# The first mixer of a two-block kernel: the convolution's projections ahead, the inverse's rows ahead of the token-major operands, fox in steps

## The chip, the cores and the metric

One core of a Trainium2 chip runs the whole kernel in one launch. The core has a matmul engine (PE, TensorE, with its weight loads shown apart as PEld), a vector engine (DVE), an activation engine (ACT), a general engine (POOL, GpSimd) and a queue engine that issues transfers (SP). Each engine works through its own list of instructions in order, and waits on semaphores for the others. The metric is the device time of one execution in microseconds, here the median over several runs. TensorE's clock is granted by the chip: 1.00 in the profile's column PEclk is 2.4 GHz, 0.50 is 1.2 GHz.

## What is computed

Two blocks one after the other on x, 256 tokens of 1024 values, in fp32. The first block has two layers, and each begins with the mixer that the change is about:

```python
def hybrid_mixer(x, w_in, mix_scale, w_out, gdn_conv_w, gdn_a_log, gdn_dt_bias, gdn_norm_w,
                 cnv_dw_w, cnv_dw_b, cnv_ln_g, cnv_ln_b, fox_f_bias):
    proj = jnp.einsum('btd,de->bte', x, w_in)
    (a_q, a_k, a_v, a_decay, a_beta, a_gate, c_glu, f_q, f_k, f_v, f_forget) = split_columns(proj, IN_SIZES)
    qkv = jax.nn.silu(causal_depthwise_conv(jnp.concatenate([a_q, a_k, a_v], -1), gdn_conv_w))
    ...
    o_a = gated_delta_rule(heads(a_q, GDN_HEADS), heads(a_k, GDN_HEADS), heads(a_v, GDN_HEADS), log_decay, beta)
    ...
    glu_a, glu_b = jnp.split(c_glu, 2, axis=-1)
    u = glu_a * jax.nn.sigmoid(glu_b)
    u = causal_depthwise_conv(u, cnv_dw_w) + cnv_dw_b          # 31 taps
    o_b = jax.nn.silu(layer_norm(u, cnv_ln_g, cnv_ln_b))
    ...
    o_c = forgetting_attention(heads(f_q, FOX_HEADS), heads(f_k, FOX_HEADS), heads(f_v, FOX_HEADS), log_f)
    mixed = jnp.concatenate([o_a, o_b, o_c], axis=-1) * mix_scale
    return jnp.einsum('bte,ed->btd', mixed, w_out)
```

Three branches share one projection: the gated delta rule with 6 heads of 64 (its per-chunk part inverts a unit lower triangular matrix of 64 x 64 and then runs a recurrence over four chunks of 64 tokens), a long depthwise convolution with 31 taps over 256 channels, and forgetting attention with 6 heads ("fox"). Behind each mixer stand layer norms and a feed-forward part, dense in the first layer and a mixture of experts in the second; the second block of two layers follows and is not touched.

## The kernel before, in words

Tokens lie along the free axis in most tiles: a projection matmul has 128 output columns of the weight as its stationary operand, and 256 tokens as the moving one. Weights come as a stream of pieces of 128 columns by SP's queue. A piece marked 'w' in `WHOLE` goes to PE as it came, in fp32 (operand `raw`, or `x,raw` in the mixer); a piece marked 'p' is split into a high part (`hi`, on ACT) and a rest (`lo`, on DVE), and takes three quicker matmuls (`xh,hi`, `xl,hi`, `xh,lo`), called projection matmuls below.

`_mixer1` (line 724) runs at 0 to 240 us for layer 0 and at 430 to 660 us for layer 1. It first projects k and q with their short convolution, then `gdn` (line 922) takes over: decays and a first gram matrix, the token-major operands `kbe`, `kd`, `vb` (keys and values transposed and scaled), then the inverse. The inverse has two parts: 16 *rows* of its 16 x 16 diagonal blocks (lines 1003 to 1021: POOL builds `dd`, PE spreads it, DVE makes a product `xpr` and sums it into `xt`, one row behind the other), and *levels* that double the block's size (from line 1024 on: transposes `cst,XT`, matmuls `xt,A`, `xc,A`, `zc,X` of 16 or 32 columns). A second pair of decays and gram matrix with q follows, then `u` and `wT` (matmuls `vb,XT` and `XT,kbe`), and the recurrence over four chunks (`S,wT`, `vn,kd`, `dec,vn`, `qg,S`). `fox` (line 1186) works head by head: scores from four operands (`cr,selt`, `selt,cr`, `mkb,identb`, `fb`), a softmax on ACT and DVE, transposes `cst,fp` and matmuls `fpT,fv`. `conv_taps` (line 1161) steps the 31 taps of the long convolution (`cvacc`, DVE), `conv_norm` (line 1174) normalizes it (`ps_st`, `ln_r`, `ln_mr`).

All other work of the mixer is put between these steps by hand. `fill(...)` (line 817) reads letters from a table `FILL`, one per layer, at marks in the code: 'c' draws the next pieces of the projection stream, a digit draws that many steps of the convolution's taps, 'U' loads and 'u' multiplies a part of the second block's memory projection (`ps_mm<-raw`). The order of the program made in this way is the priority by which a scheduler sets each engine's list. Before, `fox` is called whole behind `gdn`.

## Time and profile before

| | us |
|---|---|
| median of the runs | 2953.21 (2950.23 to 2973.36) |
| profiled execution, time | 2977.77 |
| profiled execution, span of its instructions | 2976.0 |
| PE busy | 2914.9 (98%) |
| DVE busy | 2161.2 (73%) |
| ACT busy | 1753.1 (59%) |
| POOL busy | 77.8 (3%) |

The mean granted clock of the span is 0.976. The profile is read in three steps: the busy shares and the chain tell which engine sets the end; the windows tell PE's busy time and clock in each stretch; the timeline gives the durations of single instructions. In a group like `ps_sm<-xt,A 128x16 x12` the result stands left of the arrow and the operands right; an fp32 matmul appears as two records, so x12 is six matmuls. An interval in brackets is the engine's idle time before it, with the instruction that ended it.

### The profile page before, as it was taken

The page shows a single profiled execution, that of the slowest core. Times are in us where ns is not written, and L with a number is a line of the kernel's source. Part 1 is how long each engine was busy: PE and PEld are TensorE (multiplying, and loading weights), DVE is VectorE, ACT ScalarE, POOL GpSimd, SP SyncE. Part 2 cuts the span into 40 slices and gives each one's busy share as a digit, 9 for nine tenths or more (in the row PEclk, how much of TensorE's full clock was granted, in tenths as well). Part 3 has the DMA queues.
Part 4 walks back from the last instruction along what each step waited for, and adds up shares of the span by engine and source line. Part 5 has one row for each costly group of instructions (what it writes and reads, how often), then busy time and mean ns, then how long its engine had stood idle before and what let it go on. Part 6 is the DMA issues. An engine that isn't in the chain of part 4 may idle for free.

```text
span 2976.0 us, 48787 instructions
## 1 busy us (share of the span) xinstructions
PE 2914.9 (98%) x19525; PEld 2642.4 (89%) x19525; DVE 2161.2 (73%) x3156; ACT 1753.1 (59%) x2576; POOL 77.8 (3%) x142
## 2 busy tenths in 40 slices
PE   8999999999999999999999999999999999999998
PEld 7889998888788787788888899989999999989998
DVE  5466556649888898898988866676766665767764
ACT  4245444448787776778777754565554444665543
POOL 1100001000000000000000000100000000100000
PEclk9799999899999999999999999999999999999999
DMA  5224533229989998898999755534655555435553
GB/s 196 82 103 167 200 135 114 91 79 359 361 327 357 364 356 315 335 349 343 354 364 365 269 201 186 192 107 150 217 184 187 184 186 194 146 102 197 206 186 113
DMA packets 104205, 663.77 MB, mean 223 GB/s; under 512 B 11808, under 2 KB 17952, under 8 KB 28576
## 3 DMA queue, kind: packets, MB, share of 16 engines
q1 hardware_dynamic: 101664, 658.46, 60.2%
q8 instruction: 156, 2.56, 0.3%
q10 hardware_dynamic: 2304, 2.10, 0.2%
q14 instruction: 81, 0.66, 0.1%
HBM read 657.36 MB, written 3.15 MB: 222 GB/s over the span
## 4 chain that ended last, share of the span: by engine, by line
PE 57%; DVE 2%; ACT 1%; issue 0%; POOL 0%; POOLq 0%; DVEq 0%; ACTq 0%
PE ps_mm L216 47%; PE py L216 5%; PE ps_fx L216 2%; PE ps_sm L216 2%; DVE lo L205 1%; PE ps_fx L226 0%; PE ps_sm L226 0%; DVE aa L1776 0%; ACT hi L201 0%; DVE gi L205 0%; PE ps_st L216 0%; DVE aa L205 0%; ACT xr L202 0%; DVE y L213 0%; DVE ffab L205 0%
## 5 line engine op out<-in xcount | busy, mean ns | idle before, releaser
L205 DVE TENSOR_TENSOR lo<-raw,hi 128x1024 fp32r<-128x1024 f32 (+2 forms) x1216 | 1435.1, 1207 | 392.2 <-ACT hi L201 378.4
L201 ACT ACTIVATE hi<-raw 128x1024 fp32r<-128x1024 f32 (+2 forms) x1216 | 1247.1, 1044 | 637.5 <-PE ps_mm L216 474.1
L216 PE MATMUL ps_mm<-xh,hi 128*128 128x256 f32 x2736 | 776.9, 284 | 13.2 <-ACT hi L201 8.2
L216 PE MATMUL ps_mm<-xh,lo 128*128 128x256 f32 x2736 | 771.9, 283 | 2.1 <-DVE lo L205 2.1
L216 PE MATMUL ps_mm<-xl,hi 128*128 128x256 f32 x2736 | 772.5, 282 | 0.0
L216 PEld LDWEIGHTS ps_mm<-xh,hi 128*128 128x128 f32 x2736 | 520.3, 190 | 19.4 <-ACT hi L201 8.9
L216 PEld LDWEIGHTS ps_mm<-xh,lo 128*128 128x128 f32 x2736 | 519.5, 190 | 6.0 <-issue 3.3
L216 PEld LDWEIGHTS ps_mm<-xl,hi 128*128 128x128 f32 x2736 | 520.9, 190 | 3.2 <-issue 2.9
L216 PE MATMUL ps_mm<-lo,xgh 128*128 128x512 f32 x896 | 356.8, 399 | 0.7
L216 PE MATMUL ps_mm<-hi,xgl 128*128 128x512 f32 x896 | 350.0, 391 | 0.0
L216 PE MATMUL ps_mm<-hi,xgh 128*128 128x512 f32 x896 | 349.5, 392 | 0.0
L216 PE MATMUL ps_mm<-ffl,hi 128*128 128x256 f32 x880 | 246.8, 280 | 0.0
L216 PE MATMUL ps_mm<-ffh,hi 128*128 128x256 f32 x880 | 246.7, 280 | 0.0
L216 PE MATMUL ps_mm<-ffh,lo 128*128 128x256 f32 x880 | 246.7, 280 | 0.0
L216 PEld LDWEIGHTS ps_mm<-lo,xgh 128*128 128x128 f32 x896 | 168.4, 188 | 48.5 <-DVE lo L205 16.4
L216 PEld LDWEIGHTS ps_mm<-hi,xgh 128*128 128x128 f32 x896 | 168.5, 188 | 35.6 <-ACT hi L201 0.2
L216 PEld LDWEIGHTS ps_mm<-hi,xgl 128*128 128x128 f32 x896 | 168.7, 188 | 32.4
L216 PE MATMUL py<-lo,hh 128*128 128x512 f32 x448 | 178.5, 398 | 0.5
L216 PE MATMUL py<-hi,hl 128*128 128x512 f32 x448 | 174.8, 392 | 0.5
L216 PEld LDWEIGHTS ps_mm<-ffl,hi 128*128 128x128 f32 x880 | 166.6, 189 | 0.0
L216 PEld LDWEIGHTS ps_mm<-ffh,hi 128*128 128x128 f32 x880 | 166.5, 189 | 0.0
L216 PEld LDWEIGHTS ps_mm<-ffh,lo 128*128 128x128 f32 x880 | 166.5, 189 | 0.0
(432 smaller groups left out, 3762.5 us busy)
## 6 DMA issues: line engine op xcount, KB each, us to landing
raw<-in_sm SPq DMA_DIRECT2D x336, 1024.0 KB, 6.5
raw<-in_s SPq DMA_DIRECT2D x248, 1024.0 KB, 4.8
raw<-in_s SPq DMA_DIRECT2D x40, 512.0 KB, 3.4
raw<-in_s SPq DMA_DIRECT2D x32, 256.0 KB, 2.7
raw<-in_mem SPq DMA_DIRECT2D x5, 1024.0 KB, 4.9
kv<-kvt ACTq DMA_DIRECT2D x16, 128.0 KB, 2.1
raw<-kv SPq DMA_DIRECT2D x16, 128.0 KB, 2.8
raw<-in_s SPq DMA_DIRECT2D x2, 1005.0 KB, 6.8
```

The costliest lines, as they stand in the source:

```text
L201: return self.nc.scalar.activation(out, in_, func, scale=scale, **kw)
L205: return self.nc.vector.tensor_tensor(out=out, in0=a, in1=b, op=op)
L216: return self.nc.tensor.matmul(out, lhsT=l, rhs=r, start=start, stop=stop, skip_group_check=True, **kw)
```

## The change

It replaces the two tables `FILL` by one and adds a row `REST` that is played behind `gdn`; the order of the projections changes; in `gdn` the code of the inverse's rows is moved ahead of the exponentials and transposes of the token-major operands; `fox` becomes a generator of ten steps (letter 'x') that writes its result to a tile of its own, which is split later; a tile of the softmax becomes smaller. Line numbers after are one higher from line 164 on, up to the moved code.

```diff
-FILL = ({'s': 'cccc', 'g': 'ccccccc', 'i3': 'cccc', 'f20': '3', 'f00': '2', 'v0': 'U', 'f11': '6', 's2': 'u', 'f10': '4', 's1': 'u'}, {'s': 'cccc', 'g': 'ccccccc', 's1': 'cccc8', 'i1': 'cccc', 'f21': '6', 'z': '1', 's3': 'cc8', 'w': 'u', 'i5': 'U', 's2': 'u'})
+FILL = {'s': 'cccc', 'g': 'cccccccc', 'd': 'cccccc'}
+REST = 'ccccx3cc3x3x3x3Ux3x3x3ux3x3x3ccccu999'
...
-        pp = self.ph.tile([128, 2, T], F32, name="fp", tag="fp", bufs=2)
+        n0, nn = segs[0][1], sum(n for _, n in segs)
+        pb = self.ph.tile([128, nn], F32, name="fp", tag="fp", bufs=2)
+        pp = [pb[:, :n0], pb[:, n0:]]
...
-        rest = cols('fq', 3) + cols('fk', 3) + cols('gate', 3)
-        cl = [cols('v', 3)[:2], cols('v', 3)[2:], cols('gb', 2), cols('ga', 2)] + [rest[i:i + PG] for i in range(0, 9, PG)]
+        qk = cols('fq', 3) + cols('fk', 3)
+        cl = [cols('gb', 2), cols('ga', 2), cols('v', 3)[:2], cols('v', 3)[2:]] + [qk[i:i + PG] for i in range(0, 6, PG)]
+        cl += [cols('gate', 3)[:2], cols('gate', 3)[2:]]
...
+                elif n == 'x':
+                    next(box['fox'], None)
...
+        fo = self.sb([3, T], "fo")
+        box['fox'] = self.fox(l, fq, fk, fv, logf, fo)
         oS = self.gdn(l, qkv, lr, g, lnb, fill)
-        fill('c' * 40)
-        fill('9999')
-        fill(FILL[l].get('z', ''))
-
+        fill(REST)
         mh, ml = self.new_hl()
-        self.fox(l, fq, fk, fv, logf, mh, ml, fill)
-        fill(FILL[l].get('n', ''))
+        for i in range(3):
+            self.split(mh[:, 5 + i], ml[:, 5 + i], fo[:, i])
         self.conv_norm(l, G)
...
         L = gram(decay(0, "mL", rL), k)
-        fill(FILL[l].get('d', ''))
+
+
+        six = lambda a: a.rearrange("p a i c -> p (a i) c")
...
+        self.tt(dl, d16, dl, ALU.subtract)
+        xt = self.ph.tile([128, 12, 16], F32, name="xt16", tag="xt16", bufs=1)
+        nc.vector.tensor_copy(out=xt, in_=d16)
+        fill(FILL.get('d', ''))
+        prod = self.ph.tile([128, 12 * 16], F32, name="xpr", tag="xpr", bufs=1)
+        for i0 in range(0, 16, 2):
...
 
         self.act(ex[:, :, 0:6], rL, AF.Exp)
...
-    def fox(self, l, fq, fk, fv, logf, mh, ml, fill):
+    def fox(self, l, fq, fk, fv, logf, fo):
...
+        yield
         for i in range(3):
...
                 PT.append(self.softmax_T(segs))
-                fill(FILL[l].get(f'f{i}{par}', ''))
+                yield
...
-            self.split(mh[:, 5 + i], ml[:, 5 + i], po, self.p(f"mix_scale{l}", 5 + i))
+            self.act(fo[:, i], po, AF.Copy, scale=self.p(f"mix_scale{l}", 5 + i))
+            yield
```

How the engines' lists change is shown at three places of layer 0; layer 1 is almost alike. A line is: source line, operation, result and operands, size, and how many of them follow each other.

DVE's list at the start of the inverse's rows. Before:

```order
L205 TENSOR_TENSOR xpr<-ps_sm,xt_631 128x24
L1021 TENSOR_REDUCE xt_631<-xpr 128x12
L205 TENSOR_TENSOR xpr<-ps_sm,xt_631 128x36
L1021 TENSOR_REDUCE xt_631<-xpr 128x12
L205 TENSOR_TENSOR xpr<-ps_sm,xt_631 128x48
```

DVE's list at the same place, after (`cacc` and `qkv` are the short convolution of v, `cvacc` the long one's taps):

```order
L206 TENSOR_TENSOR xpr<-ps_sm,xt_579 128x36
L214 SCALAR_TENSOR_TENSOR cacc<-craw,gch_157,cacc 128x254
L1007 TENSOR_REDUCE xt_579<-xpr 128x12
L214 SCALAR_TENSOR_TENSOR cvacc<-uu,cdwh_368,cvacc 128x250
L214 SCALAR_TENSOR_TENSOR cacc<-craw,gch_157,cacc 128x253
L206 TENSOR_TENSOR xpr<-ps_sm,xt_579 128x48
L214 SCALAR_TENSOR_TENSOR cvacc<-uu,cdwh_368,cvacc 128x249
L1007 TENSOR_REDUCE xt_579<-xpr 128x12
```

The rows stood back to back; now each product and each sum has up to two operations of the two convolutions behind it, and further down `kbe`, `kd` and `vb` stand among the last rows. On PE, 144 projection matmuls stand between the eight `dd` and ahead of the first level, where raw matmuls of the memory's projection stood.

PE's list in the levels, from the first 16-column matmuls of the second half on. Before:

```order
L226 MATMUL ps_sm<-cst,XT 128x128 x3
L216 MATMUL ps_sm<-xt_631,A 128x16 x6
L216 MATMUL ps_mm<-x,raw 128x256 x2
L216 MATMUL ps_sm<-zc,X 128x16 x6
L226 MATMUL ps_sm<-cst,XT 128x128 x3
L216 MATMUL ps_mm<-x,raw 128x256
L226 MATMUL ps_sm<-cst,XT 128x128 x3
L216 MATMUL ps_sm<-xc,A 128x32 x6
```

PE's list there, after:

```order
L217 MATMUL ps_sm<-zc,X 128x16 x6
L227 MATMUL ps_sm<-cst,XT 128x128 x3
L217 LDWEIGHTS identb
L217 MATMUL ps_mm<-mkb,identb 128x128
L217 MATMUL ps_mm<-fb 128x128
L217 MATMUL ps_mm<-cr,selt 128x256
L227 MATMUL ps_sm<-cst,XT 128x128 x3
L217 MATMUL ps_sm<-xt_579,A 128x16 x6
L217 MATMUL ps_mm<-selt,cr 128x256
```

The raw matmuls between the levels have been replaced by the four kinds of score matmuls of `fox`; two and a half heads stand in the levels, one and a half in the decays and gram that follow.

PE's list in the second gram matrix and behind it, where the levels have ended. Before:

```order
L216 MATMUL ps_sm<-qkv 128x128 x3
L216 MATMUL ps_mm<-xl,hi 128x256
L216 MATMUL ps_mm<-xh,lo 128x256
L216 MATMUL ps_sm<-rows,selt 128x256
L216 MATMUL ps_mm<-xh,hi 128x256
L216 MATMUL ps_mm<-xl,hi 128x256
L216 MATMUL ps_mm<-xh,lo 128x256
L216 MATMUL ps_mm<-xh,hi 128x256
L216 MATMUL ps_sm<-rows,selt 128x256 x2
```

PE's list there, after:

```order
L217 MATMUL ps_sm<-qkv 128x128 x6
L217 MATMUL ps_mm<-raw 128x256
L217 MATMUL ps_sm<-qkv 128x128 x3
L217 MATMUL ps_sm<-rows,selt 128x256
L227 MATMUL ps_fx<-cst,fp 128x128 x3
L217 MATMUL ps_fx<-fpT,fv 64x128
L217 MATMUL ps_sm<-rows,selt 128x256 x2
L217 MATMUL ps_fx<-fpT,fv 64x128 x2
```

Sixteen projection matmuls stood between the second decays and the `XT,kbe` matmuls; now pieces of `fox` stand there. In the recurrence that follows, 54 projection matmuls have been replaced by `cst,fp`, `fpT,fv` and 16 raw ones. The last two heads stand behind the recurrence, then the gate's 48 projection matmuls, 24 raw ones, and the convolution's statistics, with 8 projection matmuls between the last of these (`zq`) and `ln_r`.

## Rows read from the trace of the kernel before

**Rows 1.** Page, busy time (us, share, instructions) and chain by engine:
```profile
PE 2914.9 (98%) x19525; PEld 2642.4 (89%) x19525; DVE 2161.2 (73%) x3156; ACT 1753.1 (59%) x2576; POOL 77.8 (3%) x142
...
PE 57%; DVE 2%; ACT 1%; issue 0%; POOL 0%; POOLq 0%; DVEq 0%; ACTq 0%
```

**Rows 2.** Waits of PE, first and second execution: us in total, times, longest:
```profile
PE ps_sm L216 <- POOL dd L1011: 2.1, 2, 1.9
...
PE ps_sm L216 <- POOL dd L1011: 3.7, 1, 3.7
```

**Rows 3.** Windows, first execution; columns in the first row:
```profile
core 0: us, PE busy (x) PEld busy (x) DVE busy (x) ACT busy (x) POOL busy (x), PEclk, DMA share, GB/s
...
87.00:98.30 11.30, 11.30 (x83) 10.33 (x82) 4.78 (x6) 4.59 (x9) 3.95 (x2) 1.00 0.52 186
98.30:132.40 34.10, 34.10 (x136) 30.34 (x136) 12.70 (x23) 9.23 (x26) 0.00 (x0) 0.50 0.21 78
132.40:172.00 39.60, 39.60 (x333) 35.10 (x333) 30.25 (x75) 16.94 (x31) 0.00 (x0) 1.00 0.19 67
172.00:200.00 28.00, 27.27 (x176) 21.14 (x174) 15.82 (x50) 13.90 (x42) 2.06 (x3) 1.00 0.29 114
```

**Rows 4.** Windows, second execution, same columns:
```profile
505.00:521.00 16.00, 15.41 (x61) 11.21 (x62) 10.64 (x35) 2.00 (x2) 6.29 (x8) 0.80 0.40 155
...
528.00:549.00 21.00, 21.00 (x89) 19.27 (x87) 8.21 (x18) 4.21 (x10) 1.64 (x1) 0.51 0.02 5
...
603.00:617.00 14.00, 14.00 (x50) 9.80 (x51) 4.23 (x17) 4.90 (x19) 0.00 (x0) 0.52 0.10 40
```

**Rows 5.** Timeline of PE: start, duration, operation; levels at two clocks:
```profile
94.78 1.41 PE L216 MATMUL ps_sm<-xt,A 128*128 128x16 f32 x12
...
530.15 2.58 PE L216 MATMUL ps_sm<-xt,A 128*128 128x16 f32 x12
```

**Rows 6.** Timeline of DVE: operands, inverse's rows, convolution taps, a weight's split:
```profile
65.59 0.55 DVE L205 TENSOR_TENSOR kd<-ps_sm,ex 128x384 f32<-128x384 f32 x1
...
76.28 0.18 DVE L205 TENSOR_TENSOR xpr<-ps_sm,xt 128x24 f32<-128x24 f32 x1 [3.29 <-PE ps_sm L216]
...
85.85 0.35 DVE L1021 TENSOR_REDUCE xt<-xpr 128x12 f32<-128x192 f32 x1
...
162.20 10.12 DVE L213 SCALAR_TENSOR_TENSOR cvacc<-uu,cdwh,cvacc 128x239 f32<-128x239 f32 x27
...
173.52 2.35 DVE L205 TENSOR_TENSOR lo<-raw,hi 128x1024 fp32r<-128x1024 f32 x2
```

**Rows 7.** Timeline of PE: `dd`, two heads' starts in fox, projection matmuls:
```profile
78.38 0.81 PE L216 MATMUL ps_sm<-dd,cst 128*128 128x384 f32 x2
...
178.47 0.38 PE L216 MATMUL ps_mm<-cr,selt 128*128 128x256 f32 x1
...
180.50 0.38 PE L216 MATMUL ps_mm<-cr,selt 128*128 128x256 f32 x1
...
195.95 0.28 PE L216 MATMUL ps_mm<-xh,hi 128*128 128x256 f32 x1
196.07 0.28 PE L216 MATMUL ps_mm<-xl,hi 128*128 128x256 f32 x1
```

**Rows 8.** Windows, matmuls and splits of raw alone, columns as above:
```profile
87.30:98.30 11.00, 5.22 (x21) 3.49 (x20) 2.45 (x2) 2.11 (x2) 0.00 (x0) 1.00 0.53 191
98.30:116.80 18.50, 7.29 (x14) 4.09 (x14) 2.44 (x2) 2.09 (x2) 0.00 (x0) 0.50 0.23 86
```

**Rows 9.** Timeline of PE and of DVE: the convolution's statistics and norm:
```profile
176.01 0.58 PE L216 MATMUL ps_st<-cst,zq 128*128 128x1 f32 x4
...
180.09 0.16 DVE L213 SCALAR_TENSOR_TENSOR ln_mr<-ln_m,ln_r 128x2 f32<-128x2 f32 x1 [0.82 <-POOL ln_r L524]
```

**Rows 10.** Timeline of PE: operands of the delta rule, its second chunk:
```profile
133.73 1.15 PE L216 MATMUL ps_sm<-XT,kbe 128*64 128x128 f32 x12
...
145.53 0.43 PE L216 MATMUL ps_sm<-qg,S 128*128 128x64 f32 x2
```

More of the change, by code (lines that the diff above doesn't have):

```diff
@@ L705, in softmax_T @@
         for j, (s, n) in enumerate(segs):
-            self.ts(pp[:, j, :n], pp[:, j, :n], sm[:, j:j + 1], ALU.mult)
+            self.ts(pp[j], pp[j], sm[:, j:j + 1], ALU.mult)
             for kt in range(n // 128):
-                self.tr(pt[:, i], pp[:, j, kt * 128:kt * 128 + 128])
+                self.tr(pt[:, i], pp[j][:, kt * 128:kt * 128 + 128])
                 i += 1
-        sT = self.ph.tile([128, 4, 128], F32, name="fpT", tag="fpT", bufs=3)
+        sT = self.ph.tile([128, nn // 128, 128], F32, name="fpT", tag="fpT", bufs=3)
         self.act(sT[:, :i], pt[:, :i], AF.Copy)
@@ L754, in ev @@
                     if not first:
[L755 removed]
+                        fill(FILL.get(f"e{i0 + j}", ''))
             return ev
@@ L815, in _mixer1 @@
         units = list(UNITS[f"m{l}"])
+        box = {}
         def fill(p):
@@ L972, in gdn @@
         L = gram(decay(0, "mL", rL), k)
-        fill(FILL[l].get('d', ''))
+        six = lambda a: a.rearrange("p a i c -> p (a i) c")
+        mk = lambda n: self.masks[n][:, None, :].to_broadcast([128, 6, 128])
+        d16 = self.c("d16")[:, None, :].to_broadcast([128, 12, 16])
+        At = [self.g2("A", (6, 128)) for _ in range(2)]
+        dl = self.ph.tile([128, 12, 16], F32, name="dl", tag="dl", bufs=1)
+        for t in range(2):
+            self.tt(At[t], six(L[t]), mk("M_same16"), ALU.mult)
+            nc.vector.tensor_reduce(out=dl[:, 6 * t:6 * t + 6], in_=At[t].rearrange("p m (r j) -> p m j r", j=16), axis=AX.X,
+                                    op=ALU.add)
+        self.tt(dl, d16, dl, ALU.subtract)
[4 more added lines that the diff above has]
+        for i0 in range(0, 16, 2):
+            dd = self.ph.tile([128, 2, 192], F32, name="dd", tag="dd", bufs=2)
+            nc.gpsimd.tensor_tensor(out=dd, in0=dl.rearrange("p m j -> p (m j)")[:, None].to_broadcast([128, 2, 192]),
+                                    in1=self.c("d16")[:, i0:i0 + 2, None].to_broadcast([128, 2, 192]), op=ALU.mult)
+            pb = self.bank("sm", shape=(2, 12, 16))
+            self.mm(pb.rearrange("p a m j -> p (a m j)"), self.c("B16"), dd.rearrange("p a n -> p (a n)"), start=True, stop=True)
+            fill(FILL.get(f'i{i0 // 2}', ''))
+            for a in range(2):
+                i = i0 + a
+                if i:
+                    pv = prod[:, :12 * (i + 1)].rearrange("p (m j) -> p m j", m=12)
+                    self.tt(pv, pb[:, a, :, :i + 1], xt[:, :, :i + 1], ALU.mult)
+                    nc.vector.tensor_reduce(out=xt[:, :, i], in_=pv, axis=AX.X, op=ALU.add)
         self.act(ex[:, :, 0:6], rL, AF.Exp)
@@ L1059, in gdn @@
         aT = gram(decay(1, "mA", cb), q)
-        fill(FILL[l].get('a', ''))
+        fill(FILL.get('a', ''))
         qg = self.g2("qg")
@@ L1092, in gdn @@
             self.act(u[:, t], pu, AF.Copy)
-        fill(FILL[l].get('w', ''))
+        fill(FILL.get('w', ''))
         vn = self.g2("vn", (2, 3, 128))
```

53 lines of the change are left out of this document (13 added, 40 removed).

## The prediction, made before the kernel ran

> **What bounds the kernel now.** I read the page first: PE is busy for 2914.9 us, 98% of the span, and 57% of the chain that ended last is PE's own work, against 2% for DVE and 1% for ACT [rows 1]. The change moves matmuls and adds none, so the time can change in only two ways: PE idles more or less, or a stretch of PE's work runs at another clock. I therefore read two more views of the two executions of the first mixer (at 0 to 240 us and 430 to 660 us).
>
> The waits of PE show how little idle there is to win: in the first execution the largest item is 2.1 us for `dd` (the inputs of the inverse's rows, built on POOL), in the second 3.7 us [rows 2].
>
> The windows show something larger. From 98.3 to 132.4 us PE is busy for 34.10 of 34.10 us, at a granted clock of 0.50: 1.2 GHz instead of 2.4. The matmul engine had been busy without a gap before the fall. Ahead of it and behind it the clock is 1.00 [rows 3]. In the second execution the same happens at 528 to 549 us (0.51), and also at 505 to 521 us (0.80, behind the 3.7 us wait) and at 603 to 617 us (0.52) [rows 4]. What runs there: from 98.3 us and from 528 us it is the inverse's levels, short matmuls of 16 or 32 columns and transposes, with raw 256-column matmuls of the memory's projection between them; from 603 us it is `fox` alone. The same twelve 16-column matmuls take 1.41 us at full clock and 2.58 us at half [rows 5]. A busy stretch of T us at clock c loses T(1-c): 34.1 x 0.50 = 17.1 us in the first mixer; 16 x 0.20 + 21 x 0.49 + 14 x 0.48 = 3.2 + 10.3 + 6.7 = 20.2 us in the second. Together **37.3 us**, six times the two waits for `dd` together. This is the largest item that the change can touch.
>
> **The change part by part.** (1) *Operands behind the rows.* Six DVE products (`kbe`, `kd`, `vb`, about 0.47 us each, 2.8 us in all) no longer stand between the gram matrices and `dl` [rows 6]. What that is worth is not 2.8 us but only PE's idle time there, the 2.1 and 3.7 us.
>
> (2) *The rows' cover.* Before, the inverse's rows take DVE from 76.28 to 86.2 us, 10 us in which it does nothing else, and PE fills with raw matmuls [rows 6]. Now 144 projection matmuls (fq and fk: 6 groups of 8 times 3) stand among the eight `dd`. At 0.12 us each [rows 7] they are 17 us; with 8 `dd` at most 0.81 us [rows 7], 12 transposes and some small ones PE has about 24 us to do. The wait for `dd` should go: **-5.8 us**. Bound: 0 to -5.8.
>
> But DVE gets more too. By the order it now does, between its first product of the rows and its last operand, 23 taps of the long convolution at 10.12/27 = 0.375 us, 12 operations of v's short convolution (about 0.4 us, nearest row the same tap), 2 `lo` at 1.2 us, and the six operands: 8.6 + 4.8 + 2.4 + 2.8 = 18.6 us, beside some 8 us of the rows themselves (30 operations between 0.18 and 0.36 us) [rows 6]: 26.6 us against PE's 24. PE needs the last row for the levels. The excess is 0 to 6 us a mixer; I take 1.5, since some of the taps stand ahead of the first row: **+3 us** for both.
>
> (3) *The levels.* Their filler changes from raw matmuls to pieces of `fox`. PE's work in the levels is, from 87.3 to 116.8 us, 11.0 us at full and 18.5 at half, less the raw matmuls' 5.2 and 7.3: 5.8 + 11.2/2 = 11.4 us, say 12, as records overlap [rows 8]. Two and a half heads at 2.03 us [rows 7] add 5. Neither part held the clock: the levels fell with raw matmuls between them, `fox` alone fell at 603 us though not in the first mixer (172 to 200 us, [rows 3]). So I expect the fall here in both mixers. In the first mixer it came 11 us behind the levels' start (87.3 to 98.3 us, [rows 8]); with a thinner filler I take 6.5 us. Of 17 us, 10.5 then run at half and lose 10.5.
>
> (4) *When does the clock return?* Before, the first mixer went through the second decays and gram at half, and returned at 132.4 us, where 16 projection matmuls had been mixed in. 15.6 us at half there, less those 16 (0.24 each) and four raw records (0.52 each, [rows 8]), are 9.7, or 4.9 us at full. Now no projection matmul is there but 1.5 heads of `fox` (3 us). I take it that the clock returns in this stretch, about two thirds in: 5.5 more us lost. **16 us a mixer, 32 in all, instead of 37.3: -5.3 us.** At 603 us nothing is left of the old stretch: two heads run there, the others have been moved.
>
> (5) *The tail.* `fox` alone used to lie between the convolution's statistics and its norm: from the last `zq` (to 176.6 us) DVE has `ln_mr` ready at 180.25 us, and PE had all of `fox` to do before it needed it [rows 9]. Now 8 projection matmuls (1 us) stand there. 3.7 - 1.0 leaves a wait of 2.7 us, if the matmuls stand as the order has them. Bound: 0 (the chain on an idle ACT, DVE and POOL is quicker) to 4 us a mixer (the wide Silu's input is late too). I take 2.5: **+5 us** for both. This is the cover that the change gives up.
>
> (6) *At nothing.* Three more ACT copies to split `fo` and a smaller `fp` tile: ACT is 59% busy and their columns are used last. The gate's projections, now late, feed only the Silu of (5). In the delta rule 54 projection matmuls are replaced by transposes, value matmuls and 16 raw ones (0.43 us each at full clock, the pair of records); DVE's chain per chunk stays covered.
>
> Sum: -5.8 + 3 - 5.3 + 5 = -3.1 us. The profiled execution took 2977.77 us, so 2974.7 in its own terms; it lies 24.6 us above the median of the runs, 2953.21, and against that the sum is **2950 us**.
>
> **A rule against the row.** The row says: busy 34.10 of 34.10 us, clock 0.50 [rows 3]. The Trainium skill ("TensorE: Matmul & The Clock Gate", section "Why this matters for your kernels") ties a drop of throughput mid-kernel to idle gaps between bursts of matmuls. By it the levels, which no idle gap precedes in the order after, would hold 2.4 GHz; the trace disagrees, since no gap stood before 98.3 us either. Its result is rival B below.
>
> **The rivals.** *A (the forecast, 40%):* both mixers fall in the levels and return in the second gram. With (2)'s excess and (5) both at nothing it is 2942, with 4 us a mixer for each 2958.
>
> *B, no fall (17%).* For it: `fox` ran at 1.00 in the first mixer (172 to 200 us, [rows 3]); its 256-column pieces could carry the levels. Against it: 603 to 617 us [rows 4], and the levels' fall with a denser filler. In one mixer it gives 2950 - 16 = 2934 (10%), in both 2918 (7%).
>
> *C, half clock up to the raw matmuls of the delta rule (29%), the case on the other side.* For it: nothing in the second gram is as dense as the 16 projection matmuls that stood there. The work that would then be at half is 10.5 + 7.9 (all of (4)) + 10.3 (the `XT,kbe` and `vb,XT` matmuls and the first two chunks, 133.73 to 145.96 us, less 16 projection matmuls at 0.12, [rows 10]) + 2 of `fox`'s transposes = 31 us lost. Against it: 617 us, where the clock returned within `fox`. One mixer: 2950 + 15 = 2965 (15%); both: 2980 (11%); through the whole delta rule, some 10 us more each, 3000 (3%). It decides from 17.5 us lost per mixer: beyond that the kernel is slower than before. 16 is close to it, which is why I forecast no change.
>
> *D, DVE becomes the bound of the rows (9%).* The excess is 6 us a mixer rather than 1.5, and the wait costs clock as that ahead of 505.59 us did (3.2 us, the window from 505 us): 2950 + 2 x 7.7 = 2965. For it: 26.6 against 24; against it: taps can be passed by the rows where the order puts them behind.
>
> *E, the order does little (5%)*, idle and clock stay as they are: 2953.
>
> **How the numbers follow.** The predicted time is A's, 2950; its own range 2942 to 2958. From 2922 to 2980 us everything is held but B in both mixers, half of C in both and the longest C: 16 in 100 outside. One per cent (29.5 us) is about what can be told from no change here. Faster by that means below 2923.7: B in both, and some of B in one: 0.11. Slower means above 2982.7: part of C in both and the longest: 0.09. Within: 0.80.
>
> **What would show it.** Granted clock of 0.50 from within the levels to the second gram, and 1.00 behind it (A); to the delta rule (C); not at all (B). PE waiting for `XT` at the end of the rows, 1 to 2 us (D if over 5), no wait for `dd` over 1 us, and a wait for `ln_r` of 2 to 3 us in each tail. At 600 us no half clock as long as 14 us. The prediction is wrong if the clock falls already in the rows, where I count on 1.00, or if the delta rule shows PE waiting for DVE by more than 1 us a chunk.

## The result and the profile after

The kernel after takes **2994.69 us** (median of 12 executions, 2984.28 to 3005.31), the kernel before in the same rounds 2973.11 us (2949.72 to 2980.22, 12 executions). The ratio is 1.0088 with a 95% interval of 1.0065 to 1.0111: slower by nine in a thousand, and the interval leaves out 1. As a ratio that is inside the one per cent that the prediction called "within"; as a time it is 45 us above the predicted 2950, outside the range of 2922 to 2980 and past 2982.7, where the prediction let "slower" begin. The profiled execution after took 2995.4 us (span 2993.6, mean granted clock 0.974).

The page after, busy times and chain, answers to [rows 1]:

```profile
PE 2922.8 (98%) x19525; PEld 2646.5 (88%) x19525; DVE 2164.3 (72%) x3156; ACT 1755.1 (59%) x2582; POOL 82.0 (3%) x142
...
PE 57%; DVE 2%; ACT 1%; issue 0%; POOL 0%; POOLq 0%; DVEq 0%; ACTq 0%
```

PE has the same 19525 instructions and is busy 7.9 us longer. The span grew by 17.6 us against the profile before, so nearly 10 us are idle time of PE. The windows of the first mixer after, with the columns of [rows 3]:

```profile
60.00:88.00 28.00, 23.53 (x120) 17.73 (x119) 26.63 (x47) 11.97 (x32) 10.61 (x9) 0.94 0.50 188
88.00:113.00 25.00, 24.16 (x184) 21.86 (x183) 22.32 (x62) 8.54 (x20) 4.13 (x3) 1.00 0.07 22
113.00:120.00 7.00, 7.00 (x30) 5.92 (x29) 1.55 (x4) 1.32 (x4) 1.64 (x1) 0.50 0.01 2
120.00:150.00 30.00, 30.00 (x124) 25.73 (x125) 9.98 (x26) 9.20 (x32) 0.00 (x0) 0.50 0.00 1
150.00:172.00 22.00, 22.00 (x114) 17.98 (x112) 8.52 (x25) 6.48 (x18) 0.00 (x0) 0.50 0.00 0
172.00:176.00 4.00, 4.00 (x21) 2.83 (x20) 1.75 (x4) 0.64 (x2) 0.00 (x0) 0.72 0.02 4
176.00:210.00 34.00, 34.00 (x212) 26.65 (x211) 13.91 (x34) 12.21 (x29) 0.00 (x0) 1.00 0.31 107
```

The clock falls at 113 us, some five microseconds into the levels, and stays at 0.50 through the levels, the second decays and gram and half of the recurrence, until 174 us: 61 us at half clock, 30 us lost, where [rows 3] has 34.1 at half. PE is busy for 30.00 of 30.00 us meanwhile. It also falls for a few microseconds in the rows, beside the wait for `dd`: 0.94 in the window from 60 us. The second mixer, to set beside [rows 4]:

```profile
520.00:530.00 10.00, 6.93 (x22) 4.46 (x23) 10.00 (x25) 3.80 (x11) 4.94 (x6) 0.66 0.49 203
...
560.00:582.00 22.00, 22.00 (x97) 19.28 (x97) 7.83 (x20) 6.72 (x22) 0.00 (x0) 0.54 0.00 1
582.00:620.00 38.00, 38.00 (x272) 28.85 (x273) 20.12 (x58) 13.65 (x43) 0.00 (x0) 1.00 0.16 52
```

Here the same order of work runs some 20 us at half in the levels and has its clock back in the second gram. The fall in the rows is there too (0.66 in the window from 520 us), as it was in the second mixer before (0.80, [rows 4]). The half clock of `fox` alone ([rows 4], from 603 us) is gone. In PE's timeline of the first mixer the return can be placed:

```profile
114.28 2.58 PE L217 MATMUL ps_sm<-xt,A 128*128 128x16 f32 x12
...
171.41 1.06 PE L217 MATMUL ps_mm<-raw 128*128 128x256 f32 x2
...
173.88 0.84 PE L217 MATMUL ps_mm<-raw 128*128 128x256 f32 x2
```

The twelve records of 16-column matmuls take 2.58 us, the half-clock duration of [rows 5]; the full clock is back beside the first raw matmuls of the recurrence. That these brought it back is not shown by one profile. The course is that of rival C, which counted on 31 us lost, in one of the two mixers.

PE's waits after, first mixer (30 to 260 us), then the second (440 to 690 us); columns as in [rows 2]:

```profile
PE ps_sm L217 <- POOL dd L997: 3.2, 1, 3.2
...
PE ps_sm L217 <- POOL ln_r L525: 2.2, 2, 1.6
PE ps_sm L217 <- DVE xpr L206: 2.0, 5, 1.0
PE ps_sm L217 <- POOL ovr L1157: 1.8, 2, 1.1
```

```profile
PE ps_sm L217 <- POOL dd L997: 2.8, 1, 2.8
PE ps_sm L217 <- POOL ovr L1157: 2.7, 2, 2.0
PE ps_sm L217 <- POOL ln_r L525: 2.3, 2, 1.7
...
PE ps_sm L217 <- DVE xpr L206: 1.5, 1, 1.5
```

The wait for `dd`, predicted to go, is 6.0 us in all against 5.8 [rows 2]. New are the waits for `xpr` (3.5 us) and, in the tail, most of those for `ovr` (4.5 us; 1.4 before), the norm of the delta rule's heads. The kernel before had in each mixer:

```profile
PE ps_sm L216 <- POOL ovr L1152: 0.7, 1, 0.7
```

The wait for `ln_r`, which the prediction put at 2 to 3 us in each tail, is 0.59 us in the first mixer's and 0.58 in the second's; the longest one in each row above is that of another norm, which waited 1.6 to 1.7 us before too.

### The profile page after: what moved, and what is told of

Its sections match the earlier page's. It is cut to its first block, busy times and chain, and to the rows that moved or that the text cites. A ratio compares the mean times of both kernels' runs of the same rounds, so it can differ in the third digit from the quotient of the medians.

```text
span 2993.6 us, 48771 instructions
## 1 busy us (share of the span) xinstructions
PE 2922.8 (98%) x19525; PEld 2646.5 (88%) x19525; DVE 2164.3 (72%) x3156; ACT 1755.1 (59%) x2582; POOL 82.0 (3%) x142
## 4 chain that ended last, share of the span: by engine, by line
PE 57%; DVE 2%; ACT 1%; issue 0%; POOL 0%; POOLq 0%; DVEq 0%; ACTq 0%
PE ps_mm L217 46%; PE py L217 5%; PE ps_fx L217 2%; PE ps_sm L217 2%; DVE lo L206 1%; PE ps_fx L227 0%; PE ps_sm L227 0%; DVE aa L1784 0%; ACT hi L202 0%; DVE gi L206 0%; PE ps_st L217 0%; DVE aa L206 0%; ACT xr L203 0%; DVE y L214 0%; DVE ffab L206 0%
```

## The experiments

**How they are read.** Each execution has a time and a mean granted clock. I call time x (1 - clock) the *loss* to the clock, and time less loss the *rest*. Over the 146 executions of the kernel before that ran beside the experiments the time goes from 2949 to 2985 us and the loss from 38 to 78 us, while the rest stays within 2904 to 2915, 2908.4 in the mean. Time follows loss with a correlation of 0.98, 0.84 us for each us. So one profile says little on a kernel's clock, and a mean over ten or twelve executions a good deal (its uncertainty is 1.5 to 4 us). Of the ten executions of `tail_early` the two longest, 3014.63 and 3018.80 us, are not in its row; with them its loss is 82.3 us and its rest 2907.5. All means:

| kernel | executions | time | loss | rest |
|---|---|---|---|---|
| before | 146 | 2968.1 | 59.7 | 2908.4 |
| after | 12 | 2993.9 | 77.4 | 2916.6 |
| raw_gram | 12 | 2983.9 | 67.9 | 2916.0 |
| dense | 12 | 2993.7 | 81.9 | 2911.9 |
| v_first | 12 | 2977.1 | 62.5 | 2914.5 |
| tail_early | 8 | 2983.2 | 74.6 | 2908.5 |
| best_after | 6 | 2992.4 | 84.8 | 2907.6 |
| d_up | 10 | 2985.3 | 64.5 | 2920.8 |
| tail_d | 6 | 3001.3 | 91.1 | 2910.2 |
| raw_lev | 12 | 2967.5 | 48.0 | 2919.4 |
| raw_tail | 12 | 2972.2 | 58.5 | 2913.8 |
| raw_v | 10 | 2965.8 | 45.1 | 2920.7 |
| rows_first | 12 | 2977.6 | 68.0 | 2909.6 |
| mix_fox, mix_fox2 | 24 | 2961.6 | 42.9 | 2918.7 |
| mix_raw | 6 | 2994.3 | 73.4 | 2921.0 |
| mix_tail | 12 | 2973.0 | 61.2 | 2911.8 |
| mix_all | 12 | 2969.9 | 50.8 | 2919.2 |
| p_lev | 12 | 2972.9 | 68.6 | 2904.3 |

After against before is +17.7 us of loss and +8.2 us of rest: two thirds clock, one third idle time of PE (the two profiles show 10.2 us more idle in the two mixers).

### What brings the clock back, and one part of the change at a time

`raw_gram` changes after: the raw matmuls stand ahead of the later heads of `fox`.

```diff
-REST = 'ccccx3cc3x3x3x3Ux3x3x3ux3x3x3ccccu999'
+REST = 'ccccUx3cc3x3x3u3u3x3x3x3x3x3x3xcccc999'
```

> The changed kernel with one line of order changed: in the row played behind the delta rule, the load and both parts of the memory projection (the raw matmuls) come ahead of the later heads of fox instead of among the last ones. The levels keep nearly the same fox pieces; from the last level to the end of the delta rule PE now has raw 256-column matmuls between the steps where the changed kernel had fox. Theory 1 (what was lost is clock, and the clock comes back where dense matmuls stand): in the first mixer the half clock begins in the levels as before and ends in the second gram, at about 145 to 155 us instead of 174, which saves 10 to 13 us; ratio to the kernel before about 1.004 to 1.005. Theory 2 (PE's waits for dd, xpr, ln_r and ovr are the cost): they stay, so the ratio stays at 1.009. Theory 3 (the fall depends only on the levels, and its end on time): half clock to about 174 us again, ratio 1.009.

2984.0 us, ratio 1.0051 [1.0025, 1.0076]. Its profile:

```profile
110.00:139.00 29.00, 29.00 (x127) 25.77 (x127) 10.21 (x25) 7.62 (x23) 1.72 (x2) 0.53 0.00 1
139.00:160.00 21.00, 20.94 (x167) 16.41 (x167) 14.05 (x36) 7.64 (x23) 0.00 (x0) 1.00 0.08 26
```

The levels fall all the same, but the clock is back in the second gram, as expected, and the mean loss is 9.5 us lower. So the late return is one part of the loss. In the second mixer of this profile the levels run 27 us at half, against 20 in after.

`dense` changes after too: the gate's projection matmuls and the raw ones stand ahead, `fox` last and alone.

```diff
-REST = 'ccccx3cc3x3x3x3Ux3x3x3ux3x3x3ccccu999'
+REST = 'ccccUcccccccc3u3u3x3x3x3x3x3x3x3x3x3x999'
```

> The changed kernel with one line of order changed: behind the delta rule the gate's projections and both parts of the memory projection come first and all of fox last. The levels get the gate's projection matmuls (about 4 between two steps), the second gram and the delta rule the raw ones, and fox runs alone between the convolution's statistics and its norm, as in the kernel before. Theory 1 (clock): the levels fall later or for a shorter time than in the changed kernel and the clock is back in the second gram at the latest: half-clock loss of 10 to 17 us in the first mixer instead of 35; the second may lose 7 in fox again. The wait for ln_r is gone. Ratio to the kernel before 0.995 to 1.003. Theory 2 (PE's waits at the rows): only the tail's 3 to 5 us are regained, ratio about 1.007.

2993.77 us, 1.0084 [1.0058, 1.0109]. The rest fell by 4.7 us, the tail's. The clock didn't follow:

```profile
112.00:142.00 30.00, 30.00 (x147) 29.09 (x147) 10.92 (x24) 7.36 (x22) 3.28 (x2) 0.54 0.00 1
180.00:203.00 23.00, 22.77 (x88) 16.23 (x87) 6.12 (x27) 7.00 (x27) 0.70 (x1) 0.55 0.33 128
```

By its instruction list what stands between the levels here is projection matmuls, 256 columns each, and PE's weight loads are busy 29 of 30 us; it runs at half clock none the less (0.54, 27 us at half; in the second mixer 10). `fox` alone falls as it did before [rows 4]. This miss ended the idea that a denser stretch is enough.

`rows_first` moves only the inverse's rows ahead of the operands, in the kernel before; `before_look` is the kernel before unchanged.

> The kernel before with one part of the change alone: the inverse's rows stand ahead of the token-major operands; tables, projections' order and fox are as before. The order of DVE then has the rows back to back with the operands behind them. Theory 1 (the move is right and small): PE's wait for dd falls from 2.1 and 3.7 us to about 0 to 2, the clock's falls stay where they were; ratio 0.997 to 1.000. Theory 2 (the move itself costs, because raw matmuls that bridged the wait for dd now lack): the wait for dd grows to over 3 us in both mixers, ratio 1.001 to 1.004.

> The kernel before once more, unchanged, for its profile: its times lie in two groups, about 2950 and 2975 us. Theory 1 (the two groups are a matter of where the granted clock falls): this execution's half-clock loss in the two mixers, or elsewhere, differs from that of the first profile (49 us in the windows of both mixers together with their norms) in step with its time, by up to 23 us. Theory 2 (they are a matter of transfers or of the chip): the half-clock stretches are the same ones and the difference stands in PE's idle time.

`rows_first`: 2980.53 us, 1.0039 [1.0013, 1.0064]; loss +8.3, rest +1.2. The move as such gives nothing back: PE waits 2.4 and 3.6 us for `dd`, where 0 to 2 had been expected. The second profile of before (2974.08 us) was the run that corrected my reading most:

```profile
98.30:132.40 34.10, 34.03 (x265) 29.77 (x263) 20.15 (x42) 13.79 (x35) 1.14 (x1) 0.95 0.27 98
...
165.00:183.00 18.00, 18.00 (x63) 12.27 (x63) 6.62 (x26) 5.09 (x20) 0.70 (x1) 0.53 0.38 159
...
521.00:541.00 20.00, 20.00 (x83) 18.38 (x81) 7.50 (x16) 3.83 (x10) 1.64 (x1) 0.50 0.02 4
```

The 34.10 us that stood at 0.50 in [rows 3] run at 0.95 here: the first mixer's work from its levels to `XT,kbe` has 3.4 us at half instead of 34, and `fox`, which held 1.00 there, falls. It is the same program. The second mixer's falls did recur (20 us in the levels, 14 in `fox`, in both profiles). So the largest item of the prediction, 17.1 of its 37.3 us, was an item of one execution.

`v_first` gives after the old order of the projections.

```diff
-        cl = [cols('gb', 2), cols('ga', 2), cols('v', 3)[:2], cols('v', 3)[2:]] + ...
+        cl = [cols('v', 3)[:2], cols('v', 3)[2:], cols('gb', 2), cols('ga', 2)] + ...
```

> The changed kernel with the projections' old order: v ahead of the convolution's two groups. By the order, v's short convolution then stands ahead of the inverse's rows on DVE instead of among them, and 15 projection matmuls stand in the levels. Theory 1 (the time without the clock's loss grew by 8 us partly because DVE has too much to do among the rows): it falls from 2917 to 2912 to 2915; the loss by the clock stays near 77 or falls a little through the projection matmuls in the levels; ratio 1.005 to 1.008. Theory 2 (DVE in the rows is not what costs; only the tail and the clock do): time without the clock's loss 2916 to 2918, ratio 1.008 to 1.010.

2977.92 us, 1.0043 [1.0017, 1.0068]: loss -14.9, rest -2.1, and the waits for `xpr` fall from 3.5 to 1.8 us. In this kernel the new order of the projections costs some 17 us, nearly all of it clock; beside raw matmuls in the levels (`raw_v` against `raw_lev`, below) it costs 2 us, so the 17 are not a price of the order alone.

### The tail and the rows' wait

`tail_early` puts the convolution's norm ahead of the last heads of `fox`, in after.

```diff
-REST = 'ccccx3cc3x3x3x3Ux3x3x3ux3x3x3ccccu999'
+REST = 'ccccx3cc3x3x3x3x3U999'
...
+        self.conv_norm(l, G)
+        fill('xxxxuccccxxxxuccccxx')
...
-        self.conv_norm(l, G)
```

> The changed kernel with one thing moved: the convolution's taps and norm are drawn ahead of the last heads of fox and of the gate's projections, so that by the order the statistics stand in the delta rule and 7 raw, 48 projection, 8 raw and 16 raw matmuls lie between ln_r and the first use of what the norm gives. Theory 1 (of the 8 us by which the time without the clock's loss grew, 4 to 5 are the tail, where nothing covers the norm any more): that time falls from 2916.6 to 2911.5 to 2913, the waits for ln_r, xh and ovr of together some 3 us (first mixer) and 7 us (second) go down to 2 to 3 us each; the loss by the clock stays near 77; ratio 1.006 to 1.008. Theory 2 (the waits of the rows are the whole of it): the time without the clock's loss stays at 2915 to 2918.

1.0057 [1.0024, 1.0089]; the rest falls by 8.1 us, to that of before, and the waits for `ln_r` and `ovr` with it. The idle time of PE in its profile is 4.0 us below that of after, so part of the 8.1 is not seen as waits there. Where they were in after, first mixer, PE's timeline (in brackets the idle time ahead):

```profile
219.67 0.71 PE L217 MATMUL ps_sm<-cst,ln_r 128*128 128x128 f32 x4 [0.59 <-POOL ln_r L525]
223.05 1.14 PE L217 MATMUL ps_sm<-cst,ovr 128*64 128x128 f32 x12 [0.73 <-POOL ovr L1157]
228.01 1.14 PE L217 MATMUL ps_sm<-cst,ovr 128*64 128x128 f32 x12 [1.08 <-POOL ovr L1157]
```

`d_up` draws the projection matmuls of fq and fk ahead of the inverse's preparation, so that they stand ahead of the waiting `dd` and not behind it; `tail_d` adds the tail of tail_early.

> The changed kernel with one line moved: the drawing of fq's and fk's projections stands ahead of the inverse's preparation (A, dl) instead of behind it, so that by the order 52 projection matmuls stand ahead of the first dd on PE, where the changed kernel has them behind the first three. Theory 1 (the wait for dd stayed at 3.2 and 2.8 us because the matmuls that should cover it stood behind the waiting dd in PE's list): both waits fall below 0.5 us and the time without the clock's loss falls by 4 to 6, to 2911 to 2913. Theory 2 (DVE is late for dl whatever PE does, and the wait only moves to the first level's transposes): the waits for XT or xpr grow by as much, time without the clock's loss 2915 to 2918. For the clock: if its loss follows from the order as a whole and not from single places, it may be anything from 60 to 85 us here.

> The changed kernel with both moves: fq's and fk's projections ahead of the inverse's preparation (as in d_up), and the convolution's norm ahead of the last heads (as in tail_early). Theory 1 (dd and the tail are the two places where PE waits): the time without the clock's loss is 2901 to 2904, below the 2908.5 of the kernel before and the 2907.5 of tail_early. Theory 2 (the wait only moves to XT): 2906 to 2909. The total then goes by the clock: at a loss of 59 us as in the kernel before 2962, ratio 0.998; at 77 as in the changed one 2977, ratio 1.003.

`d_up`: 2986.21 us, 1.0047 [1.003, 1.0063]. The wait grew. PE, then DVE:

```profile
86.44 1.60 PE L217 MATMUL ps_sm<-dd,cst 128*128 128x384 f32 x2 [4.74 <-POOL dd L997]
```

```profile
83.51 1.79 DVE L206 TENSOR_TENSOR dl<-cst,dl 128x192 f32<-128x192 f32 x1
```

Of the 144 matmuls 52 did run ahead of the first `dd`, where after has none, but DVE, which the same order moves, took the two convolutions' operations first and made `dl` at 83.51 us instead of 76.06. The rest rose by 4.2 us, above both theories. So the place in PE's list is not enough: the chain through DVE and POOL decides. `tail_d` (3001.89 us, 1.0101 [1.0073, 1.0128]) has 10.6 us of rest less than `d_up`, still above what either theory gave, and 26.6 us more of loss.

`best_after` joins v_first, raw_gram and tail_early.

> The changed kernel with three parts put otherwise together: v's projections ahead of the convolution's (as in v_first), the raw matmuls ahead of the later heads (as in raw_gram) and the convolution's norm ahead of the last heads (as in tail_early). The inverse's rows ahead of the operands, fox in steps and its own tile stay. Theory 1 (what the change costs is these three places, each by itself): the time without the clock's loss is 2905 to 2909 and the loss 55 to 63 us, ratio 0.997 to 1.001, no slower than the kernel before. Theory 2 (the rows ahead of the operands and fox in the levels cost clock by themselves, as the 68 us of rows_first say): loss 66 to 72, ratio 1.001 to 1.004.

2993.43 us, 1.0101 [1.0072, 1.013]: the rest came out as expected, 2907.6, below before. The loss, 84.8, is above that of each of the three. The clock's costs don't add over places.

### Mixing fox into the kernel before

`mix_fox` leaves the kernel before as it is up to the end of the delta rule and plays `fox` in steps among the projection matmuls left there; `mix_fox2` is the same kernel once more.

```diff
-        fill('c' * 40)
-        fill('9999')
+        fill(MIX[l])
...
+MIX = ('cccccccc3x3cx3cx3cx3cx3x3x3x3x3xcccc999', 'cc3x3cx3cx3cx3cx3x3x3x3x3xcccc999')
```

> The kernel before with the change's fox alone: fox works in steps, writes to its own tile that is split later, and has the smaller softmax tiles; the tables, the order of the projections and the delta rule are as before. Behind the delta rule the rest of the projections is drawn up to the last of fk, then the gate's projections alternate with the heads of fox. Where the two kernels differ is only the clock's cover of fox. Theory 1 (time goes with the mean granted clock, and fox alone costs clock): the loss by the clock over all executions falls from 59 us to 50 to 56, and the time less that loss stays within 2 us of the 2909 of before; ratio 0.996 to 0.999. Theory 2 (fox in steps itself costs, by its own tile and by the convolution's norm that is no longer covered): the time without the clock's loss grows by 3 to 5 us, ratio 1.000 to 1.003.

> The same kernel as in the run mix_fox, once more, on the chip of these runs. Theory 1 (its loss of 42 us by the clock is a property of its order): 40 to 46 us again, time without it 2918 to 2919, ratio 0.997 to 0.999. Theory 2 (the 42 us were chance or that chip): loss 52 to 60, ratio 1.001 to 1.004.

2960.46 us, 0.998 [0.9957, 1.0004], and 2960.24 us, 0.9987 [0.9965, 1.0008]: 5 us under the means of before in the same rounds, each interval just reaching 1. The loss is 17 us lower, the rest 10 us higher. Windows of `mix_fox`:

```profile
87.00:160.00 73.00, 72.92 (x548) 63.69 (x547) 50.04 (x113) 30.36 (x70) 4.73 (x3) 1.00 0.32 116
...
505.00:610.00 105.00, 104.41 (x737) 87.87 (x737) 66.08 (x171) 44.34 (x115) 6.91 (x7) 0.98 0.25 91
```

PE's list of this kernel is the same, instruction by instruction, as that of before from the first one to behind the `XT,kbe` matmuls of the first mixer. The levels there ran 34.1 and 3.4 us at half clock in the two profiles of before, 0 and 3.4 in the two of this kernel. A fall in the levels isn't fixed by the list alone.

`mix_raw` takes mix_fox and moves the memory's raw matmuls from the delta rule in between the later heads; `mix_tail` covers the norm with the last heads again; `mix_all` spreads the gate's matmuls over all heads and the norm's cover.

> As the kernel before with fox in steps among the gate's projections, and besides that both raw parts of the memory projection are drawn between the later heads of fox instead of within the delta rule; by the order the projection matmuls then fill the inverse's rows and the levels (2 to 5 between two steps), and raw ones the delta rule and the later heads. Theory 1 (a stretch keeps 2.4 GHz if dense matmuls are mixed into it everywhere): the loss by the clock falls below that of the kernel before, 59 us, to 40 to 52; ratio 0.993 to 0.998. Theory 2 (the levels fall whatever fills them): the loss stays at 55 to 65, ratio 0.999 to 1.003.

> The kernel before with fox in steps among the gate's projections, as in the run mix_fox, but the convolution's norm is drawn ahead of the last heads, so that fox covers it again, and fox splits its result at once, without a tile of its own. Theory 1 (in mix_fox the clock's loss was 15 us lower than in the kernel before and 10 us were given back in the tail, by the waits for ln_r, xh and ovr): the loss by the clock is 42 to 48 us and the time without it 2909 to 2912; ratio 0.993 to 0.996, faster than both kernels. Theory 2 (fox in steps costs the 10 us anywhere, by work that is cut up): time without the clock's loss again 2917 to 2919, ratio 0.997 to 0.999. Theory 3 (the clock's gain was the waits' own doing): with the waits gone the loss is back at 55 to 60 us, ratio 0.999 to 1.001.

> As the run mix_tail, with the gate's projections spread over all six heads of fox (by the order 6 to 24 projection matmuls or 4 raw ones between two half heads) instead of the first three, and the convolution's norm ahead of the last step of fox, with 13 projection matmuls between zq and ln_r. Theory 1 (mix_tail lost 61 us by the clock because its last three heads stood alone, and mix_fox only 42 because matmuls with 2.4 GHz worth of columns stood around all heads): the loss falls to 42 to 50 us, the time without it stays at 2910 to 2914; ratio 0.994 to 0.997, faster than both kernels. Theory 2 (what lowered the loss in mix_fox were the waits in the tail, by where they put the stretches behind them): the loss stays at 57 to 63, ratio 0.999 to 1.002.

`mix_raw`, 2993.89 us, 1.01 [1.0062, 1.0138], missed the first theory by 30 us. By its list the raw matmuls had left the levels, and projection matmuls and pieces of `fox` had filled their place; the levels ran 13.7 and 33.3 us at half, and a new wait came:

```profile
PE ps_sm L227 <- DVE XT L206: 6.0, 1, 6.0
```

The 5.96 us of that wait end at 528.89 us, and it is in them, at 524.6 us, that the second mixer's clock falls. Of the falls between the levels and `XT,kbe` in all profiles, only this one and those of the second mixers of `d_up` and `tail_d` (1.6 us) have an idle gap of over 0.5 us at their start or in the 10 us ahead.

`mix_tail`: 2971.24 us, 1.0013 [0.999, 1.0035]; the rest falls by 6.9, the loss rises by 18, as its third theory had it. `mix_all`: 2969.93 us, 1.0015 [0.9989, 1.0041]. Neither beats mix_fox.

### The filler of the levels

`dense`, `mix_raw` and the rest suggested a rule. In the seven profiles that I took to have raw matmuls between the levels (two of before, rows_first, two of mix_fox, mix_tail, mix_all) the stretch from the levels to `XT,kbe` is at half clock for 0 to 34 us, 7.8 on average. One of these 14 stretches does not belong there: the second mixer of rows_first has projection matmuls between its levels, and ran 0 us at half. Without it the mean is 8.4. In the seven with `fox` there (after, raw_gram, v_first, tail_early, best_after, d_up, tail_d; some have a few projection or raw matmuls too) the first mixer's stretch averages 30.5 us (the expectation of raw_lev has 32), and none is under 23; the second mixer's has 13.7 to 40.6 us, 26.8 on average. Theory R says the filler decides, S that it doesn't.

`raw_lev` puts raw matmuls back into the levels of after: the gate's groups are taken whole and drawn there. `raw_tail` adds the tail of tail_early, `raw_v` the old order of the projections.

```diff
-FILL = {'s': 'cccc', 'g': 'cccccccc', 'd': 'cccccc'}
+FILL = {'s': 'cccc', 'g': 'cccccccc', 'd': 'cccccc', 'i6': 'cccc'}
-WHOLE = ('wwwwwppppw', 'pwwwwppppw')
+WHOLE = ('wwwwwpppww', 'pwwwwpppww')
```

> The kernel after, with the gate's three groups of columns taken whole in fp32 and drawn ahead of the levels of both mixers: raw matmuls stand between the levels' short matmuls, as in the kernel before, and fox begins in the second gram. PE gets about 1.1 us more work per mixer. Theory R (what stands between the levels decides: with raw matmuls there the stretch from the levels to the operands of the delta rule ran 7.8 us at half clock on average over seven profiles, with fox there 32 us in the first mixer): half clock in the levels under 15 us in the mean of the two mixers, mean loss to the clock 55 to 65 us instead of 77.4, time about 2980. Rival S (the kind of work between the levels doesn't matter; the kernels with fox there fell for their history ahead, the rows beside projection matmuls): levels at half for 24 us and more in both mixers, loss 75 to 85, time 2992 or more.

> As raw_lev, and the convolution's norm ahead of the last heads of fox, as in tail_early. Both theories: the time less the loss falls by about 9 us against raw_lev, to 2908 to 2911. Theory R: loss 55 to 65, time about 2968 to 2972, as fast as the kernel before. Rival S: loss 75 to 85, time 2985 or more.

> As raw_lev, with the order of the projections of the kernel before (v ahead of the long convolution). Raw matmuls stand between the levels from the second pair of 16-column matmuls on. Theory R: loss 45 to 60, below the 62.5 of v_first, time less loss 2914 to 2917, time about 2965 to 2973. Rival S: loss as in v_first or above, 62 and more, time 2978 or more.

`raw_lev`: **2966.47 us**, 0.9983 [0.9957, 1.001]. The loss falls from 77.4 to 48.0 us, below before's. `raw_v`: 2961.62 us, 0.9992 [0.9968, 1.0016], loss 45.1 against v_first's 62.5, its rest of 2920.7 above the 2914 to 2917 expected. `raw_tail`: 2972.27 us, 1.0004 [0.9983, 1.0026], loss 58.5 against 74.6; its rest falls by 5.6, not 9. All three are where R put the time or below it, and far from S. The place is less clean. The profiled execution of `raw_lev`, 2981 us and so one of its slower ones, shows

```profile
118.00:140.00 22.00, 22.00 (x96) 20.24 (x96) 9.30 (x23) 5.23 (x16) 0.00 (x0) 0.53 0.00 0
140.00:160.00 20.00, 20.00 (x165) 15.96 (x163) 9.60 (x27) 9.71 (x34) 0.00 (x0) 1.00 0.15 54
```

20.5 us at half in each mixer, more than the 15 expected, where after has 61 and 20:

```profile
548.00:566.00 18.00, 18.00 (x76) 16.61 (x77) 5.80 (x15) 3.96 (x13) 0.00 (x0) 0.51 0.00 1
```

In the profile of `raw_v` the first mixer's stretch has 27 us at half and the second's 0. In that of `raw_tail` neither has any, but the clock falls right behind it, for 31 us in the first mixer and 17 in the second:

```profile
108.00:139.00 31.00, 31.00 (x235) 27.25 (x235) 20.76 (x49) 11.83 (x36) 3.28 (x2) 1.00 0.10 35
139.00:170.00 31.00, 31.00 (x150) 25.07 (x148) 7.26 (x28) 8.44 (x26) 0.24 (x1) 0.51 0.00 1
```

With raw matmuls between them the levels *can* still fall, or hand the fall to what follows.

`p_lev` is the reverse: the kernel before, with the convolution's projections split instead of whole, so that projection matmuls fill the first mixer's levels.

```diff
-WHOLE = ('wwwwwppppw', 'pwwwwppppw')
+WHOLE = ('wwwppppppw', 'pwwppppppw')
```

> The kernel before, with the long convolution's projections (two groups of each layer) split and taken as projection matmuls instead of whole in fp32: in the first mixer projection matmuls stand between the levels where raw ones stood, in the second the levels keep raw ones. PE's work falls by about 2 us a mixer, DVE and ACT split eight more pieces a mixer. Theory R: the first mixer's levels run at half clock for 20 us or more, the second's stay at 0 to 20 us; mean loss 65 to 70 instead of 59. Rival S: no change of the first mixer's levels (0 to 14 us at half in most executions), loss 55 to 62 and time 2960 to 2968.

2974.14 us, 1.0016 [0.9996, 1.0036]: loss 68.6 as R expected, +8.9 for one mixer's levels. The first mixer's levels, in the profile:

```profile
109.00:138.00 29.00, 29.00 (x142) 28.49 (x141) 10.21 (x20) 8.20 (x22) 2.24 (x2) 0.53 0.09 35
```

The second mixer's levels, which kept raw matmuls, fell for 30.7 us too in this execution, which R did not expect:

```profile
534.00:564.00 30.00, 30.00 (x123) 27.44 (x123) 11.39 (x23) 7.43 (x21) 1.64 (x1) 0.50 0.13 40
```

The rest fell by 4.1, the price of taking columns whole.

What stands shown: exchanging the levels' filler moves the mean loss, by -29.4, -16.1 and -17.4 us where raw matmuls come in, by +8.9 where they leave one mixer. `mix_raw` (+30.5) goes the same way, though it moved raw matmuls elsewhere too and has the 6 us wait. Over all twenty profiles, the 20 stretches with mainly raw matmuls between the levels are at half for 10.4 us on average (0 to 34), the 20 with `fox` or projection matmuls there for 25.6 (0 to 45). Not shown is that the whole gain lies in the levels: the edits that bring raw matmuls in also take the gate's columns whole and put `fox` later, and one profile a kernel is too little to place a mean. Why raw matmuls do it, and why one execution falls and the next doesn't, stays open.

## Why the prediction was wrong

**The base.** The 37.3 us that the profiled execution lost at half clock in the mixers were not the program's. Its loss was about 72 us, the mean is 59.7; the other 12 us belong to that execution. The median of three that I set the sum against, 2953.21, is 15 us under the mean of 146. Both were read as properties of the kernel. So "2950" began 15 us low.

**(3) and (4), the failed step.** "Neither part held the clock", which I read from levels that fell with raw matmuls between them [rows 3], was wrong for the mean: they had fallen that time. The step took `fox` for a thinner filler of the same sort and -5.3 us. In the runs the change costs 17.7 us of loss, by an estimate from the 0.84 above some 15 us of time; rival C came in one mixer of the profile, A in the other. `raw_lev` gives all of it back. C had 29% and its mechanism, no dense matmuls in the second gram, was right for the late return (`raw_gram` -9.5); of the fall in the levels it said the same as A.

**(2), the wait for `dd`.** -5.8 was counted, +0.2 came. I summed what PE has to do among the eight `dd` and overlooked that its list has these matmuls behind the first `dd`. After:

```profile
67.74 8.04 PE L217 MATMUL ps_mm<-x,raw 128*128 128x256 f32 x36
78.98 2.93 PE L217 MATMUL ps_sm<-dd,cst 128*128 128x384 f32 x4 [3.20 <-POOL dd L997]
```

```profile
74.93 1.21 DVE L206 TENSOR_TENSOR lo<-raw,hi 128x1024 fp32r<-128x1024 f32 x1
76.06 1.78 DVE L206 TENSOR_TENSOR dl<-cst,dl 128x192 f32<-128x192 f32 x1
...
78.16 1.04 DVE L214 SCALAR_TENSOR_TENSOR cvacc<-uu,cdwh,cvacc 128x252 f32<-128x252 f32 x1
...
80.09 0.47 DVE L214 SCALAR_TENSOR_TENSOR cvacc<-uu,cdwh,cvacc 128x251 f32<-128x251 f32 x1
```

What stands ahead ends at 75.8 us; `dl`, which POOL needs, is behind a `lo` on DVE and ends at 77.8. `d_up` shows that a longer cover ahead does not help while DVE's order gives `dl` no lead. The clock fell in the rows beside this wait, in both mixers (before, in the second alone), which the prediction had named as a sign that it is wrong. The rows' own excess, +3, came as +3.5, near in size but elsewhere: PE waited for `xpr` within the rows, not for `XT` at their end.

**(5), the tail.** +5 was right in kind: `tail_early` takes 8.1 us of rest away, `raw_tail` 5.6, `tail_d` 10.6. The path was another: I priced the norm's chain to `ln_r` alone, which came at 0.6 us a mixer instead of 2.5; what is late next is `ovr`, the delta rule's norm behind it, 3.1 us more than before in the profile. So far as the size is near, that is luck.

**The rivals.** B did not come. D's waits came at 3.5 us, without its 12. The rule of the Trainium skill that I set against the row ("TensorE: Matmul & The Clock Gate", section "Why this matters for your kernels"), that throughput drops behind idle gaps, would have the levels at full clock; the profile after has them at 0.50 with PE busy 24.16 of 25.00 us ahead. The one fall in the levels that begins in an idle gap of that sort is that of the second mixer of `mix_raw`, with its 5.96 us; the short falls in the rows, beside the waits of 3.2 and 2.8 us for `dd`, agree with it too.

In sum the mean went from 2968.1 to 2993.9, +25.8 instead of -3.1. By the estimate of 15 us for the clock, 20 of the 29 us missed are the clock's and 6 the wait for `dd`; the 3 left fit the tail, 8.1 in `tail_early` against 5. With the base's 15 us that is the distance from 2950 to 2994.69.

## What to carry to other kernels

Before half-clock time enters a sum, look at the mean clock of many executions: the list here was the same, and 34 us of it ran at 0.50 in one execution, 3.4 us in the next. When work is moved, ask what it was filler or cover for; with raw matmuls between them the levels ran at half for less time in the mean, `fox` covered the norm, and neither shows as a wait before. And read which engine feeds the instruction that waits: a cover on PE is worth nothing if the move makes the feeding engine later by as much.

## What the runs showed of the hardware

- The granted clock of one program on one core varies: loss 38 to 78 us over 146 executions, times 2949 to 2985 us, the rest 2904 to 2915.
- A stretch with PE busy throughout can run at 0.50: 30.00 of 30.00 us in after, with transposes and 16- to 32-column matmuls among 256-column ones. In the twenty profiles the stretches from the levels to `XT,kbe` are at half for 25.6 us on average with split projection matmuls or `fox` between them, 10.4 with raw fp32 ones, and 0 occurs with either.
- DVE slows beside POOL: a tap of the convolution takes 1.04 us at 78.16 while POOL builds `dd` from 77.92 us, 0.47 us at 80.09 when POOL is idle; `dl` takes 1.78 us while POOL makes `A` (75.15 us, for 2.48 us), 0.36 us before, where it starts in a gap of POOL. The Trainium skill ("SBUF — State Buffer", section "Who interferes with whom") says that a DVE instruction with two SBUF inputs contends with a GpSimd instruction that reads SBUF; the trace agrees, `dl` ending 0.2 us behind `A`. POOL after, and DVE before:

```profile
75.15 2.48 POOL L1041 TENSOR_TENSOR A<-dec,mkb 128x768 f32<-128x768 f32 x1 [2.58 <-DVE dl L988]
77.92 1.96 POOL L997 TENSOR_TENSOR dd<-dl,cst 128x384 f32<-128x384 f32 x2 [0.29 <-DVE dl L206]
```

```profile
72.63 0.36 DVE L205 TENSOR_TENSOR dl<-cst,dl 128x192 f32<-128x192 f32 x1
```
